# A two-layer f32 trunk on one core: one of four weight sums moves from VectorE to a ScalarE copy and an adding transfer

## The chip, the cores and the metric

The kernel runs on one core of a Trainium2 chip. Time is device microseconds of one execution; the kernel before takes 1846.71 us, the median of three runs (1846.58 to 1846.82). Beside the times there is one execution recorded by the hardware profiler, from which all rows are taken.

The engines are named as in the profile: PE multiplies matrices (PEld are its weight loads), DVE is VectorE, ACT ScalarE, POOL GpSimd; SP issues transfers. Each engine runs its own instructions in the order in which they were written, and waits for the others through semaphores.

## The reference

Two layers over 256 tokens of width 2048, all in float32. Layer 0 mixes tokens with a convolution module, layer 1 with a latent attention. After each mixer comes the part that matters here, the MLP with 8192 hidden units:

```python
def sq_relu_mlp(h, w1, w2):
    return jnp.square(jax.nn.relu(h @ w1)) @ w2
...
        h = rms_norm(x, norm_mlp_g[layer])
        x = x + sq_relu_mlp(h, mlp_w1[layer], mlp_w2[layer])
    return rms_norm(x, final_norm_g)
```

`w1` is 2048 x 8192 and `w2` 8192 x 2048, so each MLP streams 128 MB of weights through the core.

## The kernel before, in words

**Two parts for one number.** PE multiplies in a shorter float format (float32r). Every operand is split into a high part (ACT copies and rounds it: `hi`, line 443) and the rest (DVE subtracts: `lo`, line 444); a product is then three matmuls, hi by hi, lo by hi and hi by lo (`mm3_as_is`, lines 209 to 211). ACT and DVE therefore touch every weight once each.

**The MLP's work list.** The 8192 hidden units are worked in four quarters. In each, *up units* (T in the strings of `ORDERS`) multiply 128 columns of `w1` (lines 535 and 539), and *pairs* multiply two 128-row blocks of `w2` by a pair of 512-column blocks (`na`, `nb`). While the pairs of one quarter run, the up units of the next are put between them, in orders such as `TSTSTSTOSTSTSTST`. Every unit is one transfer of 1 MB into a tile `raw`, issued on SP four units ahead, and is cut in *chunks*: an up unit in two, a pair in two or four.

**Seven products instead of eight.** A pair is a 2 x 2 block product: two blocks of tokens, two of inner rows, two of columns. A plain pair (O) takes eight products. A seven-product pair (S) takes seven, with sums of blocks on both sides, by the scheme of Strassen and Winograd. With X0, X1 the two column blocks of the first rows and X2, X3 those of the second rows (the tile `x[0]`, four slices of 128 x 512), the weight side needs four sums, kept in two tiles of two slices, each with one buffer:

- T[0] = X0 + X1 and T[1] = X0 + X2, one DVE instruction over 1024 columns (line 739)
- V[0] = T[0] + X2 (line 744)
- V[1] = V[0] + X3 (line 749)

Its four chunks are `one` (X1), `two` (X2 and X3), `t13` (T) and `t24` (V); each is split by `split_into` and then multiplied with the sums on the activation side. There are 94 such pairs: 48 in the first MLP and 46 in the second.

**What sets the order.** `stream` writes everything by hand. Before chunk n is multiplied, chunks up to n + 5 have been prepared (`prep`: their split); there are six buffers each for `hi` and `lo` (`WB`). Between the preparations `stream` puts pending steps of the up units (`todo`: adding the two halves of U, line 562, relu and square on ACT, the activation's sums on DVE and its split). After an up unit's matmuls ACT copies the accumulator out (U, line 547). The sums of a pair are made one chunk ahead of `one`: `sums` (T, line 739) ahead of the preparation of the chunk before, `more_sums` (V[0], line 744) behind it; V[1] comes with `one`. In all orders used, the unit ahead of a seven-product pair is an up unit or a plain pair, with two chunks. POOL has no instruction in the MLPs.

Of the kernel before, what the change touches and what calls it, by code (L numbers as in the profile page):

```python
# [10 lines left out]
F32 = mybir.dt.float32  # L11
# [3 lines left out]
AF = mybir.ActivationFunctionType  # L15
ALU = mybir.AluOpType
AX = mybir.AxisListType

P = 128
D = 2048  # L20
KC = D // P
T = 2
S = T * P
FF = 4 * D
NB = 512
# [62 lines left out]
def trunk_kernel(  # L88
# [26 lines left out]
    nc = tc.nc  # L115
# [28 lines left out]
    def nm(s):  # L144
        uid[0] += 1
        return f"{s}_{uid[0]}"
# [45 lines left out]
    def rows(w, k0, nk, c0, n):  # L192

        return w[k0 * P : (k0 + nk) * P, c0 : c0 + n].rearrange(
            "(j p) n -> p j n", p=P
        )
# [218 lines left out]
    NPAIR = FF // P // PARTS // 2  # L415
# [8 lines left out]
    A11, A22, A12, S3, S1, S2, S4 = range(7)  # L424
# [2 lines left out]


    class Unit:
        def __init__(self, src, nj, chunks):  # L430
            self.src, self.nj, self.chunks = src, nj, chunks

    class Chunk:
        def __init__(self, prep, run, after=(), now=None, ahead=()):
            self.prep, self.run, self.after, self.now, self.ahead = prep, run, after, now, ahead

    def hi_lo(n, at=0):
        hi = wpool.tile([P, n, NB], F32R, tag="hi", name=nm("hi"), bufs=WB)
# [7 lines left out]
    def stream(chunks, todo, blocked, pool):  # L446

        units = list(dict.fromkeys(unit for unit, _ in chunks))
        raws, parts, homes = {}, {}, {}

        def start(home):
            if len(raws) < len(units):
                unit = units[len(raws)]
                homes[unit] = home
                raws[unit] = load([unit.src], unit.nj, home)

        done = [0]

        def next_step():
            if todo and (todo[0] not in blocked or blocked[todo[0]]()):  # L460
                (todo.pop(0) or (lambda: None))()

        def prep():
            n = done[0]
            if n == len(chunks):
                return
            done[0] += 1
            unit, c = chunks[n]
            ahead = []
            if done[0] < len(chunks):  # L470
                after, i = chunks[done[0]]
                ahead = [lambda fn=fn: fn(raws[after]) for fn in after.chunks[i].ahead]
            for fn in ahead[:1]:
                fn()
            unit.chunks[c].prep(raws[unit], parts.setdefault(unit, {}))
            for fn in ahead[1:]:
                fn()
            if c == unit.last_read:
                start(homes[unit])

        for home in (None, None, None, pool):
            start(home)
        for n, (unit, c) in enumerate(chunks):
            chunk = unit.chunks[c]
            while done[0] < min(n + WB, len(chunks)):
                for _ in range(2 if len([fn for fn in todo if fn]) > 4 else 1):
                    next_step()
                prep()
            if done[0] == len(chunks):
                todo[:] = [fn for fn in todo if fn]  # L490
                for fn in todo[: 2 if n < len(chunks) - 1 else None]:
                    todo.remove(fn)
                    fn()
            chunk.run(parts[unit])
            if chunk.now is not None:
                chunk.now()
            todo += chunk.after
        while todo:
            (todo.pop(0) or (lambda: None))()

    def mlp(layer, ssq, next_gain, finish=None, before=None, last_w1=None):

        w1, w2 = mlp_w1[layer], mlp_w2[layer]
# [91 lines left out]
        def down_units(hs, q, n2, held, final):  # L595

            sevens = SEVENS[layer][q]
# [6 lines left out]
            na, nb = 2 * n2, 2 * n2 + 1  # L604
# [12 lines left out]
            def mm(name, sh, sl, mh, ml, stop):  # L617
                if name not in banks:
                    banks[name] = acc_tile()
                mm3(banks[name], sh, sl, mh, ml, name not in seen, stop)  # L620
                seen.add(name)
# [79 lines left out]
            def seven_unit(p):  # L701

                x, tt = [], []
                gh_gl = lambda f: (a[:, f, :] for a in hs[p])

                closing = final and p == last_seven

                def run(names):
                    def fn(parts):
                        for name, f, key, i in names:  # L710
                            part = parts[key]
                            mm(name, *gh_gl(f), part[0][:, i, :], part[1][:, i, :],
                               closing and (not last or name in ("P1", "Q5", "Q6", "Q7")))
                    return fn

                def close_one():
                    sums_left.append(n2)
                    kept_uv.append(mp.tile([P, 2, NB], F32, tag="W", name=nm("W"), bufs=1))
                    nc.scalar.activation(kept_uv[0][:, 0, :], banks["P1"], AF.Copy)

                def close_two():
                    for t, n in ((1, nb), (1, na)):
                        xs_add(n, banks[outs[t, n]], t)

                def close_four():
                    while todo and last:
                        (todo.pop(0) or (lambda: None))()
                    first, *others = early()
                    if not last:
                        xs_add(nb, banks["P4"], 0)  # L730
                    todo[:0] = [first, *others]

                def leave():
                    n_s[0] -= 1

                def sums(raw):
                    x.append(raw.rearrange("p j (b n) -> p (j b) n", b=2))
                    tt.extend(mp.tile([P, 2, NB], F32, tag=c, name=nm(c), bufs=1) for c in ("T", "V"))
                    nc.vector.tensor_tensor(  # L739
                        tt[0], x[0][:, 0:1, :].broadcast_to([P, 2, NB]), x[0][:, 1:3, :], op=ALU.add  # L740
                    )

                def more_sums(raw):
                    nc.vector.tensor_tensor(tt[1][:, 0, :], tt[0][:, 0, :], x[0][:, 2, :], op=ALU.add)

                def one(raw, parts):
                    parts["one"] = hi_lo(1)
                    split_into(parts["one"], x[0][:, 1:2, :])
                    nc.vector.tensor_tensor(tt[1][:, 1, :], tt[1][:, 0, :], x[0][:, 3, :], op=ALU.add)  # L749

                def two(raw, parts):
                    parts["two"] = hi_lo(2)
                    split_into(parts["two"], x[0][:, 2:4, :])

                def t13(raw, parts):
                    parts["t13"] = hi_lo(2)
                    split_into(parts["t13"], tt[0])

                def t24(raw, parts):
                    parts["t24"] = hi_lo(2)  # L760
                    split_into(parts["t24"], tt[1])

                return [
                    Chunk(one, run([("P1", A11, "one", 0)]), now=close_one if closing else None, ahead=(sums, more_sums)),
                    Chunk(
                        two, run([("Q3", S4, "two", 0), ("P2", A12, "two", 1)]),
                        now=close_two if closing and not last else None,
                    ),
                    Chunk(t13, run([("Q5", S1, "t13", 0), ("Q7", S3, "t13", 1)])),
                    Chunk(  # L770
                        t24, run([("Q6", S2, "t24", 0), ("P4", A22, "t24", 1)]),
                        now=(close_four if closing else leave if not last and n2 == q % 2 else None),
                    ),
                ], 1

            made = []
            for p in range(NPAIR):
                chunks, last_read = seven_unit(p) if p in sevens else plain_unit(p)
                unit = Unit(rows(w2, 2 * (q * NPAIR + p), 2, na * NB, 2 * NB), 2, chunks)
                unit.last_read = last_read  # L780
                made.append(unit)
            return made

        with ExitStack() as cx:
            mp = cx.enter_context(tc.tile_pool(name=f"mp{layer}", bufs=1, reuse_waits="tile"))
            todo, chunks = [], []
# [16 lines left out]
            hs, run = {}, ({}, set())  # L803
            for unit in ups(hs, 0):
                put(unit)
            for q in range(PARTS):
                now, hs = hs, {}
                more = ups(hs, q + 1) if q < PARTS - 1 else []
                for n2 in ((0, 1) if q % 2 else (1, 0)):
                    final = q == PARTS - 1 or n2 == 1 - q % 2  # L810
                    units = down_units(now, q, n2, run, final)
                    sevens = [p for p in SEVENS[layer][q]]
# [9 lines left out]
                    if final:  # L822
                        run = ({}, set())
# [7 lines left out]
    with ExitStack() as cx:  # L831
# [27 lines left out]
        raws, wjs = {}, {}  # L859
# [213 lines left out]
        with tc.manual_schedule():  # L1073
# [57 lines left out]
            for c in range(1, KC + 1):  # L1131
                n = UC * c
# [88 lines left out]
            for m in range(NP):  # L1221
# [18 lines left out]
                t, i = divmod(m, NNB)  # L1240
# [69 lines left out]
    with ExitStack() as cx:  # L1310
# [59 lines left out]
        raws, parts = {}, {}  # L1370
# [264 lines left out]
        with tc.manual_schedule():  # L1635
# [9 lines left out]
            for k in range(KC):  # L1645
                u, j = divmod(k, 2)
# [18 lines left out]
            for k in range(KC):  # L1665
                u, j = divmod(k, 4)
# [59 lines left out]
            for g in range(NG):  # L1726
                for i in range(HG):
                    h = g * HG + i

                    n = -(-len(work) // (HG - i))  # L1730
# [117 lines left out]
```

## Time and profile before

| | us |
|---|---|
| median of three runs | 1846.71 |
| the profiled execution | 1846.85 |
| its span, first to last instruction | 1845.1 |
| PE busy | 1814.8 (98%) |
| DVE busy | 1635.3 (89%) |
| ACT busy | 1206.9 (65%) |
| POOL busy | 222.9 (12%) |
| DMA of the SP queue, mean of 16 engines | 64.8% |

How to read the rows: a row of the order of time or of the chain has its start, its length, engine, line, operation and tiles, and x with a count where several are merged; in brackets stands the idle time before it and what ended it. A row of a group has the count, then busy time in us and the mean of one in ns, then the engine's idle time just before them with what ended most of it. Matmuls overlap, so the distance from one start to the next, and not the length, is PE's pace. A DVE or ACT instruction also begins to read before the one ahead of it has ended: instructions of 1.22 us follow at 1.14.

### The profile page before, as it was taken

Reading aid. Unit: us, or ns where it says so; the run is one execution under the profiler, and the core shown is the slowest. Engines: PE = TensorE matmul, PEld = TensorE weight load, DVE = VectorE, ACT = ScalarE, POOL = GpSimd, SP = SyncE. Lnnn points to the kernel's source line nnn. Section 1 sums busy time; section 2 is a strip of 40 time slices with the busy share of each in tenths; the row PEclk is TensorE's granted clock in tenths of the full one; section 3 lists DMA queues with packets and bytes.
Section 4 is the critical chain, followed back from the end, with each engine's and each line's share of the span. In section 5 each row is a group of like instructions: output and inputs, shape, how many; then the busy total and the mean of one; then the engine's idle time right before and its main releaser. Section 6 shows DMA issues by size and latency. Waiting matters only on the chain.

```text
span 1845.1 us, 28522 instructions
## 1 busy us (share of the span) xinstructions
PE 1814.8 (98%) x10768; PEld 1652.8 (90%) x10768; DVE 1635.3 (89%) x2370; ACT 1206.9 (65%) x1716; POOL 222.9 (12%) x185
## 2 busy tenths in 40 slices
PE   7999999999999999999999999999999999999998
PEld 7999888888988988888899998899898898889886
DVE  5999975789999999999987765667999999999987
ACT  5556663767667677667566765566767766767654
POOL 5999500000000000000000520000000000000000
PEclk9999999999999999999999999999999999999999
DMA  8776366757667666766646545765766766677673
GB/s 237 197 191 184 121 222 183 209 167 225 203 211 233 197 213 221 227 209 217 209 150 204 150 148 182 206 187 175 216 200 214 233 205 204 215 214 221 213 243 114
DMA packets 407113, 367.62 MB, mean 199 GB/s; under 512 B 15416, under 2 KB 351936, under 8 KB 406720
## 3 DMA queue, kind: packets, MB, share of 16 engines
q1 hardware_dynamic: 405952, 363.63, 64.8%
q10 hardware_dynamic: 1024, 2.17, 0.3%
q8 instruction: 84, 1.38, 0.3%
q14 instruction: 53, 0.43, 0.1%
HBM read 363.68 MB, written 2.10 MB: 198 GB/s over the span
## 4 chain that ended last, share of the span: by engine, by line
PE 86%; DVE 10%; issue 1%; ACT 1%; DMA 1%; SPq 0%; DVEq 0%; POOL 0%; ACTq 0%
PE acc L539 23%; PE acc L210 15%; PE acc L209 15%; PE acc L211 15%; PE acc L535 12%; DVE sum L1002 7%; PE acc L219 1%; PE acc L218 1%; PE acc L220 1%; DVE lo L444 1%; PE acc L274 1%; DMA xs<-in_x 0%; PE acc L1614 0%; DVE T L739 0%; DMA pos_i<-in_positions 0%
## 5 line engine op out<-in xcount | busy, mean ns | idle before, releaser
L444 DVE TENSOR_TENSOR lo<-raw,hi 128x1024 fp32r<-128x1024 f32 (+1 forms) x512 | 569.6, 1121 | 48.5 <-ACT hi L443 48.3
L443 ACT ACTIVATE hi<-raw 128x1024 fp32r<-128x1024 f32 (+1 forms) x512 | 477.1, 968 | 66.3 <-PE acc L210 62.3
L539 PE MATMUL acc<-xt,hi 128*128 128x512 f32 x2048 | 478.4, 380 | 2.0 <-ACT U L547 1.2
L539 PEld LDWEIGHTS acc<-xt,hi 128*128 128x128 f32 x2048 | 377.0, 189 | 50.9 <-ACT U L547 2.0
L209 PE MATMUL acc<-hi,sh 128*128 128x512 f32 x930 | 353.4, 380 | 0.0
L211 PE MATMUL acc<-lo,sh 128*128 128x512 f32 x930 | 352.5, 379 | 0.0
L210 PE MATMUL acc<-hi,sl 128*128 128x512 f32 x802 | 304.0, 379 | 0.0
L535 PEld LDWEIGHTS acc<-xt,lo 128*128 128x128 f32 x2048 | 249.1, 192 | 8.0 <-DVE lo L444 1.0
L535 PE MATMUL acc<-xt,lo 128*128 128x256 f32 x2048 | 250.5, 275 | 0.4 <-DVE lo L444 0.3
L174 ACT ACTIVATE hi<-raw 128x1024 fp32r<-128x1024 f32 (+2 forms) x184 | 179.1, 1004 | 42.8 <-PE acc L210 39.4
L211 PEld LDWEIGHTS acc<-lo,sh 128*128 128x128 f32 x930 | 175.8, 189 | 25.0
L209 PEld LDWEIGHTS acc<-hi,sh 128*128 128x128 f32 x930 | 175.8, 189 | 24.6
L175 DVE TENSOR_TENSOR lo<-raw,hi 128x1024 fp32r<-128x1024 f32 (+2 forms) x118 | 132.3, 1141 | 46.7 <-ACT hi L174 46.4
L210 PEld LDWEIGHTS acc<-hi,sl 128*128 128x128 f32 x802 | 151.6, 189 | 21.5
L1002 DVE SCALAR_TENSOR_TENSOR sum<-ub,w_dw,sum 128x256 f32<-128x256 f32 x392 | 158.8, 478 | 6.0 <-ACT sum L958 5.1
L443 ACT ACTIVATE hi<-V 128x1024 fp32r<-128x1024 f32 x94 | 99.7, 1061 | 96.4 <-DVE V L749 89.8
L175 POOL TENSOR_TENSOR lo<-raw,hi 128x1024 fp32r<-128x1024 f32 x66 | 156.4, 2383 | 22.7 <-ACT hi L174 20.5
L547 ACT ACTIVATE U<-acc 128x512 f32<-128x512 f32 x128 | 75.6, 591 | 127.4 <-PE acc L539 113.5
L218 PE MATMUL acc<-xt,hi 128*128 128x256 f32 x512 | 142.2, 278 | 0.0
L443 ACT ACTIVATE hi<-T 128x1024 fp32r<-128x1024 f32 x94 | 99.2, 1055 | 65.2 <-DVE T L739 60.8
L219 PE MATMUL acc<-xt,hi 128*128 128x256 f32 x512 | 140.9, 275 | 0.5 <-DVE xt L231 0.5
L220 PE MATMUL acc<-xt,lo 128*128 128x256 f32 x512 | 140.9, 275 | 0.0
(275 smaller groups left out, 2796.9 us busy)
## 6 DMA issues: line engine op xcount, KB each, us to landing
raw<-in_mlp_w SPq DMA_DIRECT2D x256, 1024.0 KB, 6.4
raw<-in_conv_w_pw SPq DMA_DIRECT2D x64, 512.0 KB, 5.5
raw<-in_conv_w_pw SPq DMA_DIRECT2D x16, 1024.0 KB, 5.1
raw<-in_mla_w_o SPq DMA_DIRECT2D x16, 1024.0 KB, 5.6
raw<-in_mla_w_kv_up SPq DMA_DIRECT2D x8, 1024.0 KB, 6.4
raw<-in_mla_w_in SPq DMA_DIRECT2D x8, 576.0 KB, 3.9
raw<-in_mla_w_in SPq DMA_DIRECT2D x4, 1024.0 KB, 7.1
raw<-in_mla_w_q_up SPq DMA_DIRECT2D x16, 256.0 KB, 4.1
```

Of the source, the lines that this page charges most:

```text
L174: nc.scalar.activation(hi, raw[:, js, :], AF.Copy)
L175: eng.tensor_tensor(lo, raw[:, js, :], hi.bitcast(F32), op=ALU.subtract)
L209: nc.tensor.matmul(ps, sh, mh, start=start, stop=False)
L210: nc.tensor.matmul(ps, sl, mh, start=False, stop=False)
L211: nc.tensor.matmul(ps, sh, ml, start=False, stop=stop)
L218: nc.tensor.matmul(ps, wh, alternate(th), start=start, stop=False)
L219: nc.tensor.matmul(ps, wh, alternate(tl), start=False, stop=False)
L443: nc.scalar.activation(parts[0], src, AF.Copy)
L444: nc.vector.tensor_tensor(parts[1], src, parts[0].bitcast(F32), op=ALU.subtract)
L535: nc.tensor.matmul(ps[0][:, :S], wl[:, j, :], alternate(xh(k)), start=False, stop=False)
L539: nc.tensor.matmul(ps[0], wh[:, j, :], xhl(k).rearrange("p (g a b) -> p g b a", g=2, a=2), start=k == 0, stop=k == KC - 1,)
L1002: nc.vector.scalar_tensor_tensor(out=out, in0=ubs[c][:, w : w + S], scalar=tap(c, w), in1=pcs[c], op0=ALU.mult, op1=ALU.add)
```

## The change

In a seven-product pair T[1] = X0 + X2 is no longer made by DVE. ACT copies X0 into T[1], and a transfer issued on POOL's queue reads X2 again from `w2` in HBM (128 rows of 512 numbers) and adds it to what T[1] holds. Both are written two chunks ahead of `one`, in a new list `far` of a chunk. DVE's instruction shrinks to T[0] = X0 + X1 over 512 columns and stays where it was. T is taken two chunks ahead, V one chunk ahead.

`last_part` swaps the order of a preparation and the sums ahead where the chunk prepared is the last (`t24`) of a seven-product pair and the next one has sums of its own.

```diff
-        def __init__(self, prep, run, after=(), now=None, ahead=()):
-            self.prep, self.run, self.after, self.now, self.ahead = prep, run, after, now, ahead
+        def __init__(self, prep, run, after=(), now=None, ahead=(), far=()):
+            self.prep, self.run, self.after, self.now, self.ahead, self.far = prep, run, after, now, ahead, far
...
-            for fn in ahead[:1]:
+            n_first = 0 if unit.last_part == c else 1
+            for fn in ahead[:n_first]:
                 fn()
             unit.chunks[c].prep(raws[unit], parts.setdefault(unit, {}))
-            for fn in ahead[1:]:
+            for fn in ahead[n_first:]:
                 fn()
+            if done[0] + 1 < len(chunks):
+                after, i = chunks[done[0] + 1]
+                for fn in after.chunks[i].far:
+                    fn(raws[after])
...
+                src = rows(w2, 2 * (q * NPAIR + p), 2, na * NB, 2 * NB)
...
+                def third_sum(raw):
+                    x.append(raw.rearrange("p j (b n) -> p (j b) n", b=2))
+                    tt.append(mp.tile([P, 2, NB], F32, tag="T", name=nm("T"), bufs=1))
+                    nc.scalar.activation(tt[0][:, 1, :], x[0][:, 0, :], AF.Copy)
+                    nc.gpsimd.dma_start(tt[0][:, 1, :], src[:, 1, :NB], accum_op=ALU.add)
+
                 def sums(raw):
-                    x.append(raw.rearrange("p j (b n) -> p (j b) n", b=2))
-                    tt.extend(mp.tile([P, 2, NB], F32, tag=c, name=nm(c), bufs=1) for c in ("T", "V"))
-                    nc.vector.tensor_tensor(
-                        tt[0], x[0][:, 0:1, :].broadcast_to([P, 2, NB]), x[0][:, 1:3, :], op=ALU.add
-                    )
+                    tt.append(mp.tile([P, 2, NB], F32, tag="V", name=nm("V"), bufs=1))
+                    nc.vector.tensor_tensor(tt[0][:, 0, :], x[0][:, 0, :], x[0][:, 1, :], op=ALU.add)
...
-                    Chunk(one, run([("P1", A11, "one", 0)]), now=close_one if closing else None, ahead=(sums, more_sums)),
+                    Chunk(one, run([("P1", A11, "one", 0)]), now=close_one if closing else None, ahead=(sums, more_sums), far=(third_sum,)),
...
+                unit.last_part = 3 if p in sevens else None
```

More of the change, by code (lines that the diff above doesn't have):

```diff
@@ L429, in trunk_kernel @@
     class Unit:
+        last_part = None
         def __init__(self, src, nj, chunks):
```

## The prediction

> **What bounds the kernel now.** I read the page's shares first, then the busy time by stretches, the pace of TensorE in the chain that ended last, and what TensorE waited for. The page's busy shares and slices:
>
> ```profile
> PE 1814.8 (98%) x10768; PEld 1652.8 (90%) x10768; DVE 1635.3 (89%) x2370; ACT 1206.9 (65%) x1716; POOL 222.9 (12%) x185
> ...
> PE   7999999999999999999999999999999999999998
> ...
> DVE  5999975789999999999987765667999999999987
> ...
> POOL 5999500000000000000000520000000000000000
> ```
>
> The two MLPs are slices 8 to 20 and 26 to 40: PE and DVE are both full there, and POOL does nothing. Busy time in two stretches of the first MLP (columns: us, then PE, PEld, DVE, ACT, POOL busy, granted clock, DMA share, GB/s):
>
> ```profile
> 480.00:640.00 160.00, 160.00 (x866) 143.65 (x865) 159.49 (x188) 111.24 (x136) 0.00 (x0) 1.00 0.69 215
> 640.00:800.00 160.00, 160.00 (x866) 143.66 (x865) 159.49 (x187) 110.92 (x135) 0.00 (x0) 1.00 0.69 213
> ```
>
> PE has no idle time and DVE 0.51 us in 160. A busy PE may still be slowed, so the chain's pieces say at what pace it ran:
>
> ```profile
> 569.14 1.89 PE acc L535 x16
> ...
> 577.29 1.73 PE acc L539 x8
> 579.02 1.78 PE acc L535 x16
> ...
> 726.90 1.89 PE acc L535 x16
> ```
>
> Sixteen 256-column products take 1.78 us everywhere and 1.89 in two places: 0.11 us lost each time. In the second MLP a third one is at 1.92 (0.14 lost), in the same view:
>
> ```profile
> 1614.01 1.92 PE acc L535 x16
> ```
>
> PE's own order of time shows the larger losses, where the first seven-product pairs begin:
>
> ```profile
> 407.87 0.38 PE L210 MATMUL acc<-hi,sl 128*128 128x512 f32 x1
> 408.09 0.38 PE L211 MATMUL acc<-lo,sh 128*128 128x512 f32 x1
> 409.07 1.99 PE L539 MATMUL acc<-xt,hi 128*128 128x512 f32 x8 [0.60 <-ACT U L547]
> 410.90 1.05 PE L535 MATMUL acc<-xt,lo 128*128 128x256 f32 x8
> 412.11 1.16 PE L535 MATMUL acc<-xt,lo 128*128 128x256 f32 x8 [0.16 <-DVE lo L444]
> 413.11 1.25 PE L539 MATMUL acc<-xt,hi 128*128 128x512 f32 x5
> ...
> 1295.90 1.99 PE L539 MATMUL acc<-xt,hi 128*128 128x512 f32 x8 [0.60 <-ACT U L547]
> ...
> 1455.82 2.32 PE L535 MATMUL acc<-xt,lo 128*128 128x256 f32 x16
> 1457.97 1.25 PE L539 MATMUL acc<-xt,hi 128*128 128x512 f32 x5
> ```
>
> From 408.09 to 409.07 is 0.98 where the step is 0.22: 0.76 lost. Eight L539 take 1.83 instead of 1.73, eight L535 1.21 and 1.00 instead of 0.89. Sum 1.29 us. The second MLP repeats it at 1295 (1.29) and loses 2.15 - 1.78 = 0.37 at 1456. So the MLPs' own losses are 2 x 1.29 + 0.37 + 0.36 = **3.3 us**: PE at its pace is the bound, and DVE follows so closely that it ends a few waits. No relief of DVE can give back more than 3.3 us.
>
> **The change part by part.** Groups by form:
>
> ```profile
> L739 DVE TENSOR_TENSOR T<-raw 128x1024 f32<-128x1024 f32 x94 | 114.5, 1218 | 0.0
> L744 DVE TENSOR_TENSOR V<-T,raw 128x512 f32<-128x512 f32 x94 | 64.4, 685 | 0.0
> L443 ACT ACTIVATE hi<-raw 128x1024 fp32r<-128x1024 f32 x418 | 432.5, 1047 | 63.2 <-PE acc L210 59.3 <-DVE W L641 1.5 <-PE acc L539 1.0
> L443 ACT ACTIVATE hi<-raw 128x512 fp32r<-128x512 f32 x94 | 58.0, 617 | 3.1 <-PE acc L210 3.1
> L443 ACT ACTIVATE hi<-T 128x1024 fp32r<-128x1024 f32 x94 | 99.2, 1055 | 65.2 <-DVE T L739 60.8 <-PE acc L210 2.4 <-DVE lo L444 1.8
> ```
>
> *Removed:* half of each of 94 T sums. 1218 ns becomes the 685 of the same operation on 512 columns, so **DVE loses 0.53 us x 94 = 50 us of work**. It lies beside a full PE, so it is worth only what it takes from the 3.3 us.
>
> *Added on ACT:* 94 copies of 128x512, priced by the `hi<-raw` row of that size: 0.62 us x 94 = 58 us. ACT has 49 us free in 160; fourteen copies take 9 of them, so it costs nothing by volume. But ACT runs in order, and behind each copy stand the eviction U (L547), the splits of the next chunks and the forms' split. The first U is where PE waited at 409.07: there the copy comes directly ahead of it and could add 0.6 us, once a layer. ACT was late there because DVE was (its square root waits for DVE's norm), and DVE will be 0.53 earlier, so I count 0; the ends are 0 and +1.2 us.
>
> *Added wait on ACT:* T has one buffer, so the copy waits until DVE has split the last pair's T. *Added wait at the T split:* the addition must have landed. Only T's second half depends on it; DVE's first half and both V sums don't. This is the part that can cost, so I lay it along one tight cycle:
>
> ```profile
> 690.78 1.22 DVE L444 TENSOR_TENSOR lo<-T,hi 128x1024 fp32r<-128x1024 f32 x1
> ...
> 700.99 1.22 DVE L444 TENSOR_TENSOR lo<-T,hi 128x1024 fp32r<-128x1024 f32 x1
> ...
> 705.40 1.22 DVE L739 TENSOR_TENSOR T<-raw 128x1024 f32<-128x1024 f32 x1
> ...
> 710.61 1.22 DVE L444 TENSOR_TENSOR lo<-T,hi 128x1024 fp32r<-128x1024 f32 x1
> ...
> 720.82 1.22 DVE L444 TENSOR_TENSOR lo<-T,hi 128x1024 fp32r<-128x1024 f32 x1
> ...
> 730.44 1.22 DVE L444 TENSOR_TENSOR lo<-T,hi 128x1024 fp32r<-128x1024 f32 x1
> ```
>
> ```profile
> 700.01 1.04 ACT L443 ACTIVATE hi<-raw 128x1024 fp32r<-128x1024 f32 x1
> 701.13 0.60 ACT L547 ACTIVATE U<-acc 128x512 f32<-128x512 f32 x1
> ...
> 706.73 1.07 ACT L443 ACTIVATE hi<-T 128x1024 fp32r<-128x1024 f32 x1 [1.74 <-DVE T L739]
> 709.67 1.06 ACT L443 ACTIVATE hi<-V 128x1024 fp32r<-128x1024 f32 x1 [1.88 <-DVE V L749]
> ```
>
> The copy stands after ACT's split at 700.01, but T is free only at 700.99 + 1.22 = 702.21; it ends at 702.83. U moves from 701.13 to there, 1.7 us later; PE feels that only when the next up unit wants a bank, one pair on (21 products at a step of 0.22: 4.6 us). If the landing comes L us after the copy, ACT splits T in 1.07 and DVE takes over. DVE would be there at 710.61 - 0.53 = 710.08, so nothing is late while L is under 710.08 - 1.07 - 702.83 = **6.2 us**. In general the round trip is 1.22 + 0.62 + L + 1.07 = L + 2.9, against cycles of 10.21, 9.62, 10.21 and 9.62 us less 0.53 each. At L = 7.0 the 9.62 cycles each lose 0.8 and the 10.21 ones 0.2: 2.0, about the 2.1 that DVE gained in the four. So the **break-even is L near 7 us**.
>
> What is L? No row has a transfer that POOL issues, or one that adds. The nearest, in us from issue to landing:
>
> ```profile
> raw<-in_mlp_w SPq DMA_DIRECT2D x256, 1024.0 KB, 6.4
> raw<-in_conv_w_pw SPq DMA_DIRECT2D x64, 512.0 KB, 5.5
> ...
> out<-xs SPq DMA_DIRECT2D x8, 256.0 KB, 2.8
> ```
>
> ```profile
> L1325 POOL TENSOR_TENSOR m<-scratch,sin 128x128 f32<-128x128 f32 x8 | 10.2, 1278 | 0.0
> ```
>
> The size is 128 x 512 x 4 = 256 KB. Lower end: 2.8 us, as a plain transfer, POOL's work nothing. Upper end: 6.4 us, as slow as four times the bytes, plus 1.3 us of POOL's work priced by its ordinary instruction: 7.7. An addition touches its bytes at both ends, so I lean on the 512 KB row, 5.5, but transfers in that row also queued behind each other; with some POOL work I take **L = 5.5**, which is 0.7 under what the tight cycle allows. Cost: 0, hidden behind ACT's and DVE's splits of the chunks between; if that cover is gone, DVE is late, and next PE.
>
> [...]
>
> *DMA volume:* 94 x 256 KB = 25 MB more beside a share of 0.69 in the stretches above; the weights come four units ahead, and the splits of raw chunks (the 128x1024 row) waited for PE's buffers, not for a transfer. Cost 0. The transfers pass nothing on SP's queue, and POOL's is empty. The reordering of the sums ahead (n_first) changes nothing: in all orders a pair follows an up unit or a plain pair, whose chunk has no sums to swap. The raw tile's first reader comes two chunks earlier, long after its load.
>
> *Sum:* the DVE-ended losses go: 0.32 + 0.11 twice, 0.37, and 0.36, together 1.6 us. At the first pairs (409 to 417) PE follows DVE closely, and a landing 5.5 us after the copy leaves the T split hardly in time; I give back 0.4. So -1.2 us on the profiled execution's 1846.85, which stands 0.14 over the median of 1846.71: **1845.6 us**. The likeliest case's own range: all 3.3 gained (1843.5) to 1.2 lost at U and some at the first pairs (1848.5).
>
> **The rivals.**
> *Slower, the landing comes too late.* The place is the loop of T's single buffer, the price what L exceeds 7. All 94 transfers can pay it; long cycles, with a plain pair or two up units between, pay less: if only half pay, 47 us per us. L = 7.7 (the upper end): 0.7 x 47 = 33 us, 1880. Just over 7: 1850 to 1860. For it: DMA at 0.69 in the same stretches, and DVE with 0.5 us free in 160. Against: L must exceed what a four times larger load takes.
>
> *Slower, POOL held up by DVE.* If POOL can't issue while DVE works, it waits for a gap, and the stretches show none: two or three instructions of 1.2 us later, L = 5.5 + 2.4 to 3.6 = 7.9 to 9.1, which is 0.9 to 2.1 over: 42 to 99 us, 1890 to 1945. Against: POOL's slices are full at the start, beside a DVE that is also full. [...]
>
> *Faster by more than expected.* Relief of DVE widens its lead, every loss above vanishes, ACT is earlier too: 3.3 us, 1843.5. More than that PE's pace forbids, unless the start or end of the run shortens; nothing of the change lies there.
>
> *The change doesn't decouple.* If DVE's half of T had to wait for the transfer into the other half, DVE would stand still from 705.40 to about 702.83 + 5.5 = 708.3: 2.9 - 0.5 = 2.4 us x 94 = 225 us, 2071. For it: one tile, two writers. Against: they write disjoint halves.
>
> **How the numbers follow.** 0.2% is 3.7 us, about what a measurement of this kernel can tell from no change. Hidden, as forecast: 0.66, within 1843.5 to 1848.5. Landing too late: 0.17. POOL held up: 0.07. Not decoupled: 0.03. Faster by all of the 3.3 and more: 0.07, of which 0.06 beyond 0.2%, for what the records may not show. Faster 0.06; slower 0.17 + 0.07 + 0.03 = 0.27, of which some 0.01 stays within; same the rest, 0.68. The range runs from 1843.2 to 1872, which takes in the milder late landings and leaves out some 0.05 below and 0.15 above.
>
> **What would show it.** Right: the T sum at 685 ns x94; an ACT group of 0.62 us x94 writing T; a POOL queue of 94 transfers of 256 KB with a landing under 7 us; DVE idle in the 160 us stretches grown by some 7 us; PE at 1.73 and 1.78 throughout. Wrong: waits of ACT's T split for the transfer, with DVE's split of T idle behind it and PE pieces over 1.78 in every cycle; or DVE's T sum itself waiting.

## The result: one per cent slower

The changed kernel takes 1864.56 us, the median of four runs (1863.02 to 1867.01), beside 1846.64 for the kernel before in the same job. The ratio is 1.0098, with an interval of 1.0086 to 1.0111. The forecast was no change, 1845.6 us. The profiled execution of the changed kernel is the longest of the four, 1867.01 us with a span of 1865.2; that is 20.1 us more span than before. In its rows the split is at lines 445 and 446, the up unit's eviction U at 554, the copy at 747, the transfer at 748 and DVE's half of the T sum at 752.

The work went where it was meant to. From the page of the changed kernel (shares, a DMA queue, transfers with their KB and median us to landing), and then its groups by form:

```profile
PE 1820.9 (98%) x10768; PEld 1654.7 (89%) x10768; DVE 1593.7 (85%) x2370; ACT 1251.9 (67%) x1810; POOL 305.2 (16%) x279
...
q0 software_dynamic: 13536, 24.65, 7.6%
...
raw<-in_mlp_w SPq DMA_DIRECT2D x256, 1024.0 KB, 6.6
...
T<-in_mlp_w POOLq DMA_DIRECT2D x94, 256.0 KB, 5.5
```

```profile
L752 DVE TENSOR_TENSOR T<-raw 128x512 f32<-128x512 f32 x94 | 64.2, 683 | 0.0
...
L747 ACT ACTIVATE T<-raw 128x512 f32<-128x512 f32 x94 | 58.2, 619 | 12.3 <-DVE lo L446 11.9 <-DMA raw<-in_mlp_w 0.3
...
L446 DVE TENSOR_TENSOR lo<-T,hi 128x1024 fp32r<-128x1024 f32 x94 | 114.6, 1219 | 23.9 <-ACT hi L445 23.5
```

```profile
480.00:640.00 160.00, 159.09 (x866) 142.67 (x866) 152.20 (x186) 116.14 (x149) 12.19 (x14) 1.00 0.84 236
640.00:800.00 160.00, 159.50 (x864) 142.96 (x863) 152.72 (x187) 116.84 (x149) 12.23 (x14) 1.00 0.82 234
```

The last two rows are the two 160-us stretches of before. DVE's idle time in them grew from 0.51 to 7.80 and 7.28 us, nearly the forecast 7. But PE, which had none, is idle 0.91 and 0.50 us. The waits of the changed kernel say for what (us in all, times, longest; three rows of two engines):

```profile
PE acc L209 <- ACT U L554: 14.5, 10, 3.6
...
ACT hi L445 <- DMA T<-in_mlp_w: 133.9, 57, 5.7
...
ACT T L747 <- DVE lo L446: 11.9, 18, 1.6
```

The first row is new, and it is ten stalls and not 94. PE's idle time at them is 14.5 us, and its busy time grew by 1820.9 - 1814.8 = 6.1: together 20.6, which is the 20.1 within half a microsecond. One of the ten, in order of time, ACT first, then POOL, then PE:

```profile
578.74 0.62 ACT L747 ACTIVATE T<-raw 128x512 f32<-128x512 f32 x1
...
580.45 2.51 ACT L445 ACTIVATE hi<-raw 128x1024 fp32r<-128x1024 f32 x3
587.34 1.06 ACT L445 ACTIVATE hi<-T 128x1024 fp32r<-128x1024 f32 x1 [4.38 <-DMA T<-in_mlp_w]
588.30 0.58 ACT L554 ACTIVATE U<-acc 128x512 f32<-128x512 f32 x1
```

```profile
579.76 0.86 POOL L748 DMA_DIRECT2D T<-in_mlp_w  x1 [11.81 <-ACT T L747]
```

```profile
585.92 0.38 PE L209 MATMUL acc<-hi,gh 128*128 128x512 f32 x1
...
587.65 0.38 PE L211 MATMUL acc<-lo,gh 128*128 128x512 f32 x1
588.93 0.48 PE L209 MATMUL acc<-hi,gh 128*128 128x512 f32 x1 [0.91 <-ACT U L554]
```

Here an up unit is followed by a plain pair and that by a seven-product pair, which happens once in each pass of an order, twelve times in all. ACT has nothing to do from 582.96 on but waits 4.38 us, because the next instruction in its order is the T split, and T's addition has not landed. Behind that split stands U, the up unit's eviction, whose accumulator is done when the plain pair begins, at 585.92. The plain pair wants that bank as its fourth: nine matmuls fill three banks, and the tenth is due 1.94 us after the first (the distance in the rows of before below), at 587.86. It starts at 588.93. The same place in the kernel before, ACT and then PE:

```profile
580.42 1.05 ACT L443 ACTIVATE hi<-T 128x1024 fp32r<-128x1024 f32 x1
...
582.57 0.60 ACT L547 ACTIVATE U<-acc 128x512 f32<-128x512 f32 x1 [1.11 <-PE acc L539]
```

```profile
582.37 0.38 PE L209 MATMUL acc<-hi,gh 128*128 128x512 f32 x1
...
584.31 0.38 PE L209 MATMUL acc<-hi,gh 128*128 128x512 f32 x1
```

The T split was over and ACT idle when U became possible, and the tenth matmul came on time, 1.94 us after the first. U had about 1.1 us to spare there, and nothing in a busy row shows that.

### The profile page after: what moved, and what is told of

It is laid out like the page before. It is cut to its first block, busy times and chain, and to the rows that moved or that the text cites. A ratio compares the mean times of both kernels' runs of the same rounds, so it can differ in the third digit from the quotient of the medians.

```text
span 1865.2 us, 28764 instructions
## 1 busy us (share of the span) xinstructions
PE 1820.9 (98%) x10768; PEld 1654.7 (89%) x10768; DVE 1593.7 (85%) x2370; ACT 1251.9 (67%) x1810; POOL 305.2 (16%) x279
## 3 DMA queue, kind: packets, MB, share of 16 engines
q0 software_dynamic: 13536, 24.65, 7.6%
## 5 line engine op out<-in xcount | busy, mean ns | idle before, releaser
L546 PE MATMUL acc<-xt,hi 128*128 128x512 f32 x2048 | 478.4, 380 | 1.7 <-ACT U L554 1.2
L546 PEld LDWEIGHTS acc<-xt,hi 128*128 128x128 f32 x2048 | 377.0, 189 | 50.5 <-ACT U L554 2.0
L209 PE MATMUL acc<-hi,sh 128*128 128x512 f32 x930 | 353.4, 380 | 0.0
L748 POOL DMA_DIRECT2D T<-in_mlp_w x94 | 82.0, 873 | 1353.6 <-ACT T L747 1230.9
L209 PEld LDWEIGHTS acc<-hi,sh 128*128 128x128 f32 x930 | 175.8, 189 | 24.6
```

The source lines that it names most:

```text
L209: nc.tensor.matmul(ps, sh, mh, start=start, stop=False)
L546: nc.tensor.matmul(ps[0], wh[:, j, :], xhl(k).rearrange("p (g a b) -> p g b a", g=2, a=2), start=k == 0, stop=k == KC - 1,)
```

## The experiments

**The wait, or its volume.** Two kernels take the two halves of the suspected chain apart. One writes U ahead of the T split at the twelve places, by preparing one chunk less ahead there:

```diff
-            while done[0] < min(n + WB, len(chunks)):
+            late = (...)  # in words: an up unit's second chunk, and the next unit is a plain pair
+            while done[0] < min(n + WB - late, len(chunks)):
```

> The changed kernel in its own order; only at the twelve up units that stand directly ahead of a plain pair one chunk less is prepared before the unit's matmuls are written, so that ACT's queue has the eviction U ahead of the split of T and not behind it. Theory: the waits of L209 for U go, 1844 to 1847. Rival (loop of T's buffer or traffic): 1858 to 1866. If only the place of U in the queue counts, the landings stay as long as they are (4 to 9 us).

Measured: 1845.98 us (1845.62 to 1846.46), ratio 0.9997 (0.9988 to 1.0006). The landings are nearly as before the edit (4.1, 5.2 and 8.8 us at least, in the median and at most, for 4.0, 5.5 and 8.8), and the wait of L209 for U is gone. At nine of the twelve places the transfer's first packet still starts 3.8 to 5.1 us after its issue. At the place shown above ACT now has:

```profile
581.74 0.60 ACT L555 ACTIVATE U<-acc 128x512 f32<-128x512 f32 x1 [3.16 <-PE acc L547]
582.68 1.06 ACT L445 ACTIVATE hi<-T 128x1024 fp32r<-128x1024 f32 x1 [0.35 <-DMA T<-in_mlp_w]
```

So all of the loss hangs on U standing behind the T split: a late landing alone costs next to nothing. The changed kernel shows it too, for ten of its transfers at other places start 3.4 to 4.9 us after their issue and no matmul waits there for U. The same edit on the kernel before is its control:

> Control: the kernel before with the eviction written ahead of the T split at the same twelve places. Theory: there that split waits for DVE's sum by at most 2 us and no matmul waited for an eviction at a plain pair, so nothing moves, 1845.8 to 1847.2. If the order of the eviction is worth something by itself, 1845 or less.

Measured: 1846.71 us (1846.38 to 1847.01), ratio 1.0001 (0.9992 to 1.0011). The edit is worth nothing by itself.

The other keeps the copy and leaves out the transfer, and with it the addition of X2 to T[1]:

```diff
-                    nc.gpsimd.dma_start(tt[0][:, 1, :], src[:, 1, :NB], accum_op=ALU.add)
```

> The changed kernel without the adding transfer: T[1] stays a copy of X0, the addition of X2 is left out; ACT's copies stay. Theory (the wait for the transfer is the cause): 1843.5 to 1846. Rival (the 94 copies of 0.62 us on ACT in front of the evictions are the cause): it stays at 1855 to 1866.

Measured: 1845.04 us (1844.75 to 1845.18), ratio 0.9992 (0.9983 to 1.0001). The kernel before took 1846.49 in the same job. ACT's 58 us of copies cost nothing, and the relief of DVE, with no transfer in its way, is worth about 1.5 us. Everything that the change loses comes with the transfer; that it is the wait and not the traffic is what the run with U first shows, where all 94 transfers stay.

**Another order, and what its control says.** I moved the plain pair in each order from behind an up unit to ahead of it, so that it follows a seven-product pair:

```diff
-ORDERS = "STSTSTOSTSTSTSTT", "TSTSTSTOSTSTSTST"
+ORDERS = "STSTSOTSTSTSTSTT", "TSTSTSOTSTSTSTST"
```

> The changed kernel with the plain pair moved one place: STSTSOTSTSTSTSTT and TSTSTSOTSTSTSTST, so that it stands behind a seven-product pair and not between an up unit and a seven-product pair. All transfers, copies and waits for them stay. Theory (PE stalls at ten of twelve plain pairs because the eviction U of the up unit just ahead is queued on ACT behind the split of T that waits for the transfer, and the plain pair's fourth product wants that bank 1.9 us later; three long stalls also halve the clock for 3.4 us): the ten waits of L209 for U go, 20 us come back, 1843.5 to 1846.5. Rival (the late landings hold up DVE in the loop of T's one buffer, or the 25 MB disturb the weights, everywhere): nothing of that changes, 1858 to 1866.

> The kernel before with the same move of the plain pair, as control for the order: by both theories within 1.5 us of the kernel before, 1845 to 1848, since there no split waits for a transfer.

Measured: 1930.11 us, ratio 1.0447 (1.0429 to 1.0464), and 1925.66 us for the kernel before with the same orders, ratio 1.0429 (1.0414 to 1.0445). Both theories missed the first: the new orders alone cost 79 us. The plain pair now comes ahead of an up unit, and the bank that this unit wants has to be emptied of the plain pair's sums by DVE. The waits of the kernel before with the new orders, and the shares of its page:

```profile
PE acc L539 <- DVE xs L613: 51.2, 12, 5.4
```

```profile
PE 1841.8 (96%) x10768; PEld 1669.3 (87%) x10768; DVE 1638.6 (85%) x2370; ACT 1209.4 (63%) x1716; POOL 223.0 (12%) x185
```

Twelve waits of 51.2 us and 1841.8 - 1814.8 = 27.0 us more busy time make 78.2, which is the span's growth (1923.2 less 1845.1 is 78.1). The changed kernel has twelve such waits of 58.0 us, and none of L209 for U, as the theory said; but with a loss four times as large in both kernels, this pair of runs can't decide about the transfer. It shows how tight the hand-over of a bank is here, whether ACT empties it (waits of up to 3.6 us) or DVE (up to 5.4).

**Where the late landing comes from.** L is 5.5 us in the median, as forecast, yet the T split waits up to 5.7. Records of single packets say why. At ten of the twelve places the first packet of the adding transfer starts 4.3 to 5.1 us after POOL's issue and the last ends after 6.6 to 8.3; at the two without a stall these are 1.6 and 4.7 to 4.8. The DMA view from just after SP's issue of a weight load at 579.17 to 584.0, for the transfer that POOL issued at 579.76:

```profile
DMA packets 320, 0.97 MB, mean 203 GB/s; under 512 B 8, under 2 KB 96, under 8 KB 319
...
q1 hardware_dynamic: 319, 0.96, 77.1%
q8 instruction: 1, 0.02, 1.7%
```

Not one packet of POOL's queue (q0) ran in 4.2 us, while SP's queue (q1) moved 0.96 MB. Of its 319 packets 96 are under 2 KB, left from the load before; the other 223 are of 4 KB, and the load has 256 of them. So most of a weight load went ahead. Three kernels ask what of this matters.

Copy and transfer three chunks ahead, not two:

```diff
-            if done[0] + 1 < len(chunks):
-                after, i = chunks[done[0] + 1]
+            if done[0] + 2 < len(chunks):
+                after, i = chunks[done[0] + 2]
```

> The changed kernel in its own order, with the copy and the transfer begun three chunks ahead instead of two. Theory (at the twelve places up unit, plain pair, seven-product pair the landing comes 7 to 9 us after the copy, because a weight load was issued just ahead of it, and the eviction stands behind the wait): one chunk more is 1 to 2.5 us at these places, so stalls of 0.5 to 2.3 us go and the two or three longest shrink; 1846 to 1852. Rival (the wait for T's one buffer ahead of the copy): the copy now stands right behind the last pair's T split in ACT's queue, waits there in nearly every pair, and the time stays or grows, 1862 to 1880.

Measured: 1844.91 us (1844.34 to 1848.60), ratio 0.9995 (0.9986 to 1.0004), better than expected. The landings are 4.1, 5.0 and 7.9 us: the transfers came earlier, and at eleven of the twelve places also started at once, 1.6 to 1.7 us after the issue. One stall is left, where the start took 4.1. The waits of PE, then of ACT:

```profile
PE acc L209 <- ACT U L554: 0.9, 1, 0.9
```

```profile
ACT T L747 <- DVE lo L446: 66.7, 55, 2.6
```

The second row is the loop of T's single buffer, which now does hold the copy, at no cost to PE.

The transfer without its addition, so that T[1] is X2 alone (X0 is left out of the sum):

```diff
-                    nc.gpsimd.dma_start(tt[0][:, 1, :], src[:, 1, :NB], accum_op=ALU.add)
+                    nc.gpsimd.dma_start(tt[0][:, 1, :], src[:, 1, :NB])
```

> The changed kernel with the transfer as a plain one on the same queue: T[1] becomes X2 alone, the addition of X0 is left out. It prices the addition by itself: if adding is what makes the landing long, the packets' stretch falls from 2.2 us to about 1.2 and the median landing from 5.5 to about 4.3, and the time falls by 5 us or more; if the queueing behind weight loads makes it, landing and time stay within 0.5 us and 5 us.

Measured: 1845.23 us, a single run, with 1846.39 before. Its queue and its transfers:

```profile
q0 software_dynamic: 7520, 24.65, 3.7%
...
T<-in_mlp_w POOLq DMA_DIRECT2D x94, 256.0 KB, 4.5
```

The same bytes take about half the packets (7520 for 13536) and half the queue's time (3.7% for 7.6%), POOL's instruction 0.54 us for 0.86, and the landing 4.5 us for 5.5. So the addition costs about 1.0 us a transfer (the least and the most are 3.2 and 7.3 us, for 4.0 and 8.8). No matmul waits for U here, but the addition is not the only reason. At six of the twelve places the transfer still starts 3.7 to 3.8 us after its issue and lands after 5.9 to 6.1, in time; at the other six SP's load no longer falls together with it, and it starts after 1.2 to 1.3.

Then (the text in brackets stands for some lines) the weight load that I took to be in the way, written behind the copy and the transfer instead of ahead of them, still on SP's queue:

```diff
             if c == unit.last_read:
-                start(homes[unit])
+                (ahead of a plain pair: kept, and started after the next chunk's far list)
```

> The changed kernel in its own order of work; only at the twelve places (up unit, plain pair, seven-product pair) the weight load that stood directly ahead of the pair's copy and transfer is issued behind them. Theory (the adding transfer's packets start 4 to 5 us after its issue there, not 1.6, because that load's packets are ahead of them in the DMA engines): the packets start at about 1.6 to 2.5, the landing comes near 4 to 5 us, the stalls at the plain pairs go or shrink to a fifth; 1844 to 1849. Rival (the transfers are slow there for another reason): 1860 to 1867.

Measured: 1864.67 us (1858.63 to 1870.03), ratio 1.0087 (1.0070 to 1.0104), nothing gained:

```profile
PE acc L209 <- ACT U L559: 15.8, 10, 3.7
```

The place in the written order isn't the cause. The trace shows the reason: SP and POOL are separate queues (q1 and q0 above), and SP issues the load when its buffer comes free, which is when DVE has split the up unit's second chunk (579.15 in the changed kernel, the load's issue at 579.17; 580.19 and 580.22 here). The question was left whether this load is the cause at all. The last kernel therefore, on top of this edit, gives the same twelve loads to POOL, in order behind the adding transfer:

```diff
             if held:
-                start(held.pop())
+                start(held.pop(), nc.gpsimd)
```

> The changed kernel, but at the twelve places the 1 MB weight load that becomes free to start just then (its buffer is released by VectorE's split of the up unit's second chunk, which ends within a few tenths of a microsecond of POOL's issue of the adding transfer) is issued by POOL, in order behind that transfer, instead of by SP. All else stays. Theory (the transfer starts late there because a weight load's packets got in ahead of it): with the load forced behind, the adding transfer's packets begin some 1.6 us after its issue at all twelve places, landing 4 to 5 us, the evictions no longer hold the plain pairs' fourth product, and the time is that of the kernel whose evictions were moved, 1845 to 1847 us; the load starts some 2 us later, which its four units of lead hide. Rival (something else at these places makes the transfer late, such as the packets of loads already under way, or POOL itself): the packets begin 4 us and more after the issue at ten of the twelve, the waits on U stay at some 14 us, and the time stays at 1862 to 1868.

Measured: 1845.61 us (1845.18 to 1845.91), ratio 0.9994 (0.9984 to 1.0003). At all twelve places the first packet starts 1.56 to 1.61 us after the issue and the last ends after 3.8 to 4.8, and no stall of L209 of more than 0.3 us is left. POOL at the place shown above, and the median landings (the additions, and the loads on POOL):

```profile
575.20 0.86 POOL L753 DMA_DIRECT2D T<-in_mlp_w  x1 [11.17 <-ACT T L752]
576.04 0.76 POOL L164 DMA_DIRECT2D raw<-in_mlp_w  x1
```

```profile
T<-in_mlp_w POOLq DMA_DIRECT2D x94, 256.0 KB, 5.0
...
raw<-in_mlp_w POOLq DMA_DIRECT2D x12, 1024.0 KB, 7.9
```

That settles it: twelve loads of 256, ten of which got in ahead of their neighbour, make the landings late where it costs. The loads themselves take 7.9 us to land, for the 6.6 of the changed kernel's loads, and no engine that computes waits for them.

**Is there anything to win?** Three chunks ahead together with the eviction ahead of the T split (both diffs above):

> The changed kernel with both: the copy and the transfer three chunks ahead, and the eviction ahead of the T split at the twelve places. Theory: the one stall left with three chunks (1.2 us) and the ones left with the eviction first (0.9 us) go, 1843.3 to 1844.9. Rival (the two changes take the same microseconds, or the copy's wait for T's buffer holds up ACT): 1844.9 to 1846.5.

Measured: 1844.92 us (1844.02 to 1846.15), ratio 0.9992 (0.9984 to 1.0001), no more than with three chunks ahead alone. And the freed DVE time spent on one more seven-product pair in each pass of the last quarter of the second MLP, with the eviction moved; its control is the kernel before with the same pair (and without the eviction's move):

```diff
-SEVENS = (... for last in ((0, 2, 4), (0, 2)))
+SEVENS = (... for last in ((0, 2, 4), (0, 2, 4)))
-LATE_G = ((3, 5, 6, 7), (3, 4, 5, 6, 7))
+LATE_G = ((3, 5, 6, 7), (3, 5, 6, 7))
```

> The kernel with the eviction ahead of the T split (as in the run before, 1845.98 us), and one plain pair of the second MLP's last quarter made a seven-product pair, as in the first MLP: two units of 5.18 us of matmuls become two of 4.53. Theory (TensorE is the bound and VectorE has 6 us free in 160): 1.3 us less, 1844.2 to 1845.2. Rival (VectorE or the transfer's loop binds there): 1846 to 1849.

> The kernel before with the same plain pair made a seven-product pair, as control: if VectorE's relief is what makes room for it, no gain here, 1846 to 1850; if the last quarter had room anyway, 1845 to 1845.8.

Measured: 1848.23 us, ratio 1.0011 (1.0002 to 1.0020), and 1848.57 us, ratio 1.0012 (1.0003 to 1.0021). The forecast gain of both is missed. Against the kernel with only the eviction moved, the last matmul ends 0.83 us earlier (1834.29 for 1835.12), but the work after it takes 12.07 us instead of 9.07, and the span grows from 1844.2 to 1846.4. The traces show where: with only the eviction moved, four of the eight output transfers are issued at 1831.1 to 1832.6, ahead of the last matmul's end, and now at 1836.0 to 1837.5, behind it. The same four come late in the control (1836.4 to 1837.9). So the closing work of half of the output moved from beside PE to behind it, and cost more than the pair saved. No version here beats the kernel before by more than 0.1%, and all intervals of those that gain reach to 1.

## Why the prediction was wrong

*PE at its pace is the bound, with a ceiling of 3.3 us for the gain.* Right. With the cause removed in four ways the kernels take 1844.9 to 1846.0, and without the transfer 1845.04. That is 0.5 to 1.5 us less than the kernel before in the same job, though each interval reaches 1; the sum's -1.2 us for a hidden transfer lies among them. (1846.71 less 1.2 is 1845.5, and not 1845.6, which changes nothing.)

*DVE loses 0.53 us x 94.* Right: 683 ns for 1218, and the idle time grew by 7.

*94 copies cost nothing by volume.* Right: 619 ns each, 58.2 us, and no cost without the transfer. U at the first pairs of a layer was not made later: the stall ahead of L546, 0.6 us, is there twice as before.

*L = 5.5.* The size was right as a median, 5.5 with 4.0 to 8.8 from POOL's issue, and 5.9 from the copy's end, from which the prediction counts (0.40 lie between the two). What failed is to reason with one value: L isn't spread at random but is 6.9 to 8.8 at ten of the twelve places, because the load that it collides with is released by DVE at the same point of the pattern. The DMA share of 0.69, which I took for room at cost 0, didn't show it. That an addition costs more than its bytes, on which the choice of the 512 KB row leaned, the plain transfer showed only afterwards, with 4.5 us for the 5.5.

*The added wait at the T split.* This is the step that failed. The prediction followed T and DVE around the loop of the buffer and found a break-even near L = 7, which holds: the copy waits for the buffer 11.9 us in all and DVE's T split for ACT 23.5 us, and PE sees nothing of either. But for what is queued on ACT it looked only behind the copy, not behind the T split that waits for the landing. It said of U that "PE feels that only when the next up unit wants a bank, one pair on", 21 products or 4.6 us away. Where a seven-product pair follows the up unit no stall shows. Where a plain pair does, PE wants U's bank after nine matmuls, 1.94 us, and the T split of the pair behind stands ahead of U. The tight cycle that was laid out, from 690 to 730, holds no plain pair. Ten places at 1.45 us of idle time, and 6.1 us of busy time at a lower clock (0.51 to 0.52 over 3.50 us at the three longest stalls) and in the restarts (the first matmul takes 0.48 us or more, for 0.38), is the price that was put at 0.

*Of the rivals*, "the landing comes too late" (0.17) had the right cause, and the wrong place and price: not 47 us per microsecond over 7 at all pairs through DVE, but 20 us at ten places through an eviction. POOL wasn't held up: its instruction takes 0.86 us beside a DVE busy 95% of the stretch. DVE's T sum never waited for the transfer (0.0 in its row), so the two halves of T do decouple. The result lies in the range by luck, since the late landing was in it with another place and price; the point and the chance of 0.68 for no change were wrong.

## What to carry to other kernels

Where an engine that works in order gets a new wait (here ACT, for which PE stood still for 14.5 us at ten places), list every instruction behind the waiting one, at every place of the pattern where the order differs, and for each the moment at which its reader wants it; the cycle that is tightest for the bound engine isn't the one that is tightest for the queue. A latency used in such a sum should be its value at that place, next to the transfers that start there (6.9 to 8.8 us here), and not a median (5.5). If the transfers of two queues compete, as here, either give the small one a head start (one chunk more: 1844.91 us) or put both on one queue in the order that is wanted (1845.61 us).

## What of the hardware was not expected

**Most of a load went ahead.** At the ten places the 256 KB transfer on POOL's queue didn't share the engines half and half with the 1 MB load that SP issued at nearly the same time: it started 4.3 to 5.1 us after its issue, instead of 1.6, with 174 to 233 of the load's 256 packets ahead of its first. SP's issue lies between 0.6 us before POOL's and 0.3 behind it there, and 0.60 and 1.30 us behind it at the two places without a stall; only the order of the two was tested, not a threshold between 0.3 and 0.6. Why the load goes ahead is not shown: no run here shows in what order a single engine serves the two queues.

**The clock fell by fixed stretches, not by the length of a stall.** PE in the changed kernel, at one of the longer stalls and behind it, with the granted clock of a stretch of 3.5 us (the number behind POOL's busy time):

```profile
428.42 0.48 PE L209 MATMUL acc<-hi,gh 128*128 128x512 f32 x1 [2.39 <-ACT U L554]
...
429.52 0.63 PE L210 MATMUL acc<-hi,gl 128*128 128x512 f32 x1
429.95 0.63 PE L211 MATMUL acc<-lo,gh 128*128 128x512 f32 x1
```

```profile
429.20:432.70 3.50, 3.50 (x10) 2.75 (x9) 3.36 (x3) 2.42 (x4) 0.73 (x1) 0.51 0.73 279
```

Matmuls follow at 0.43 us instead of 0.22 for 3.41 us. Three of the ten stalls did this, of 2.10, 2.39 and 3.64 us; by the halved pace each cost an estimate of another 1.7 us, half of 3.41, together 5.1 of the 6.1 us of PE's added busy time. A stall of 1.92 us did not. But the length doesn't decide. In the kernel with the load written behind the transfer, a stall of 1.88 us halved the clock and one of 2.31 us did not:

```profile
675.76 0.48 PE L209 MATMUL acc<-hi,gh 128*128 128x512 f32 x1 [1.88 <-ACT U L559]
...
1418.72 0.48 PE L209 MATMUL acc<-hi,gh 128*128 128x512 f32 x1 [2.31 <-ACT U L559]
```

```profile
673.01:676.42 3.41, 1.53 (x8) 1.03 (x7) 1.54 (x3) 2.25 (x3) 0.00 (x0) 1.00 1.17 319
676.42:679.83 3.41, 3.41 (x10) 2.69 (x9) 2.94 (x4) 2.85 (x5) 0.86 (x1) 0.50 0.77 294
1417.11:1420.52 3.41, 1.80 (x8) 1.61 (x9) 2.30 (x3) 3.39 (x5) 0.00 (x0) 1.00 1.12 338
1420.52:1423.93 3.41, 3.41 (x17) 2.98 (x17) 3.41 (x5) 3.18 (x6) 0.86 (x1) 1.00 0.62 196
```

In the changed kernel the changes of the clock lie on a grid of 3.41 us (those at 429.24 and 1412.27 are 288 steps apart). The stretches above are cut by the same step (676.42 and 1420.52 are 218 apart). The first stall lies within one stretch of that grid, which is idle for 1.88 us; the second starts in the stretch before, and 1.61 us of it fall into this one. In the MLPs of the changed kernel the stretches with up to 1.30 us idle were not followed by half clock, among them the two that share the stall of 1.92 us (0.62 and 1.30), and the three with 2.10 to 3.23 us were. So a stretch of 3.41 us wasn't idle from end to end when the clock fell after it: here 1.88 us were enough, and 1.61 were not.

**The adding transfer cost more than its bytes.** Beside the plain one of the same size: packets of 2 KB for 4 KB, 0.32 us more of POOL (0.86 for 0.54), about 1.0 us more to the landing (5.5 for 4.5).
